# Sums, diagonals and spreads of the turned token groups one block ahead, and the next scaled block in front of the last one's low part

## The chip, the cores and the metric

The kernel runs on one core of a Trainium2 chip. Its time is the device time of one launch in microseconds, the median of several runs. The trace shows one profiled execution of the same program; its span runs from the first to the last instruction, and the launch's own time is a little longer.

## What is computed

One layer of a diffusion backbone: 1024 latent tokens and 256 context tokens of width 1024, all float32. The change works at the very beginning, where tokens are normalised, modulated and multiplied by the first 512 columns of the input projection (the attention values):

```python
m_lat = silu(c) @ w_mod + b_mod          # shift sh1, scale sc1, ... of the latents
m_ctx = silu(c_ctx) @ w_mod + b_mod      # the same for the context
h_lat = rms_norm(x, norm1_g) * (1.0 + sc1) + sh1
h_ctx = rms_norm(ctx, norm1_g) * (1.0 + csc1) + csh1
p_lat = h_lat @ w_in                     # columns split into the heads of retention and attention
p_ctx = h_ctx @ w_in
# retention in two directions, differential attention, output projection, residual,
# then norm, gated MLP with a depthwise convolution, residual, final norm
```

`rms_norm` divides a token by the root of the mean square over its 1024 features.

## The kernel before

Matmul operands are split into a high part, rounded to TensorE's fp32r type, and a low part, the rounding's rest. Each product is three passes: high by high, high by low, low by high (`passes`, L132 to L134; in the first stage L664, L666 and L670 of `part_products`). The modulated tokens stand with features on partitions: eight blocks `d` of 128 features in `hT[0]` (high) and `hT[1]` (low), each in two tiles of 512 tokens; `cT` holds the context.

The 1024 latents come in two ways. **The first 512** (row tiles t=0 to 3) are loaded token by token, scaled by their root, transposed on TensorE for each block (`modulate`, L570), and modulated with high part on ACT (L573), a copy `tmp` on DVE (L575) and the low part on DVE or GpSimd (L577). **The rest** is loaded already turned, features on partitions, in three groups `g` of 256 tokens: g=0 and 1 are latents 512 to 1023, g=2 is the context. For such a group the squares must be summed over partitions, and the result spread over all of them:

- `squares(g, i)`: ACT squares half of the group's eight blocks (L585, 128x1024).
- `over_blocks(g)`: DVE adds the eight blocks up in three steps (L589, L590, L591).
- `over_rows(g)`: TensorE sums over partitions against a tile of ones (`ss`, L596), DVE takes the mean (L114), GpSimd the power −0.5 (L115).
- `halves(g)`: DVE multiplies the identity by those numbers, two diagonal matrices (`diag`, L604).
- `spread(g)`: TensorE multiplies ones by the diagonals, so each partition gets every token's factor (`rp`, L608), and ACT copies that to `rr` (L609).
- `turned` (L611 on), for each block `d`: DVE scales the block by the modulation and by `rr` (L615, to `tmp` where d is even, to `u` where it is odd), ACT adds the shift and rounds (`hi`, L616). Where d is odd, ACT also adds the shift in place (L618) and GpSimd subtracts (L619); where d is even, DVE does both in one operation (`lo`, L621).

The main loop runs over the eight blocks `k` of 128 features. For each it multiplies tiles t=0, 1 (`part_products((0, 1), k)`), then tiles 2, 3, with five PSUM tiles in turn, and the calls around them prepare the blocks to come. After it, tiles t=4, 5 are multiplied block by block, with the helper `between(t, k)` behind each block: it prepares group 1 (at t=4) and the context (at t=5). Tiles 6, 7 and the context's two tiles follow (`natural`), and then block 5 of the projection, whose weights are loaded, split by ACT (L188) and DVE (L189), in four slices of two feature blocks.

Everything from `begin` to `in_order(begin)` keeps its written order on TensorE, DVE, ACT and SP: each instruction there is tied to the one before it on its engine. GpSimd and all later code are placed by the scheduler, which may also put later instructions between the tied ones. Every engine runs its queue in order, so one that waits holds back all behind it. SP issues the loads and stores; the `wr` pool has two buffers for raw weights, and `st`, from which results are stored, has two.

Of the kernel before, what the change touches and what calls it, by code (L numbers as in the profile page):

```python
# [68 lines left out]
def r32(ap):  # L69
    return ap.bitcast(F32)  # L70
# [3 lines left out]
def kernel(  # L74
# [80 lines left out]
    with ExitStack() as p1:  # L155
# [371 lines left out]
        with ExitStack() as p0:  # L527
# [83 lines left out]
            def turned(src, g, d, who, hi, lo):  # L611
# [5 lines left out]
                if d % 2:  # L617
                    nc.scalar.activation(u, u, AF.Identity, bias=sh)  # L618
                    nc.gpsimd.tensor_tensor(out=lo, in0=u, in1=r32(hi), op=ALU.subtract)  # L619
                else:  # L620
                    nc.vector.scalar_tensor_tensor(out=lo, in0=u, scalar=sh, in1=r32(hi), op0=ALU.add, op1=ALU.subtract)  # L621

            def turned_latents(g, d):
# [3 lines left out]
            def context(d):  # L627
                turned(xc[d // 4][:, d % 4, :], 2, d, 1, cT[0][:, d, :], cT[1][:, d, :])
# [5 lines left out]
            rr = xp.tile([P, 3, GQ], F32, name="rr")  # L634
            sqs, diag = {}, {}

# [88 lines left out]
            for k in range(KD):  # L725
# [19 lines left out]
                if k == 4:  # L745
                    over_rows(0)
                if k == 5:
                    spread(0)
                    squares(1, 0)
                if k >= 6:  # L750
                    turned_latents(0, 3 * k - 16)
                    turned_latents(0, 3 * k - 15)
                if k == 7:
                    halves(1)
                if 0 < k < 5:
# [12 lines left out]
                if 0 < k < KD - 2:  # L768
                    mod_sums(k + 2)
                    latents(k + 2)  # L770
                    if 0 < k < 5:
                        for q in range(2):
                            mod_part(k + 3, q)
                        mod_row(k + 3)
                if k in (0, 2, 4):
                    w_split()
                if k == 2:
                    squares(0, 0)
                if k == 4:
                    halves(0)  # L780
                if k == 5:
# [3 lines left out]
                    for i in range(2):  # L785
                        xc.append(xp.tile([P, 4, GQ], F32, name="xc", tag="wt", bufs=5))
                        turned_load(2, i)
                    squares(1, 1)
                    turned_latents(0, 0)
                    turned_latents(0, 1)  # L790
                    over_blocks(1)
                if k >= 6:
                    turned_latents(0, 3 * k - 14)
                if k == 6:
                    over_rows(1)
                if k == 7:
                    spread(1)
            rtab = load_rope(1)
# [3 lines left out]
            def between(t, k):  # L802
# [9 lines left out]
                if t == 5:  # L812
# [6 lines left out]
                    for d in ((k - 4,), range(3, KD))[k == 7] if k > 3 else ():  # L819
                        context(d)  # L820

            for t in (4, 5):
# [899 lines left out]
```

## Time and profile before

| what | us |
|---|---|
| median of 3 runs | 1397.24 (1396.67 to 1398.96) |
| the profiled execution | 1396.65 |
| its span | 1394.9 |
| TensorE busy | 1364.0 (98%) |
| DVE busy | 1003.7 (72%) |
| ACT busy | 743.1 (53%) |
| GpSimd busy | 305.3 (22%) |
| first stage, to the first matmul of block 5 of the projection | 101.0, TensorE busy 87.5 of it |

In the lines of the profile PE is TensorE's matmul, PEld its weight load, POOL is GpSimd, SPq is SP's queue of issues. A line of the timeline has the start, the duration, engine, source line, operation and tiles, and in brackets how long the engine was idle before it and whose result ended that. TensorE's clock can be granted in part; it is given as a share of full speed. Matmuls are pipelined, so that the starts count and not the ends.

### The profile page before, as it was taken

To read this page: it belongs to the slowest core of one execution; us is meant where nothing else is said; L and a number is where in the kernel's file an instruction comes from. 1 tells how busy PE (TensorE), PEld (TensorE's weight loads), DVE (VectorE), ACT (ScalarE), POOL (GpSimd) and SP (SyncE) were. 2 spreads that over 40 slices of the span, in tenths; PEclk is the share of its full clock that TensorE was granted. 3 is DMA by queue.
4 is the path that set the end of the run, shared out by engine and by line. 5 is a ranking of instruction groups with operands and counts; after the bars stand their busy time and mean duration, and the time that the engine had idled before them with its cause. 6 is when DMAs were issued, how large, how long until landed. Compare 5 with 4: busy or idle time off the path is not lost. (4 is left out here: it accounts for less than half of the span.)

```text
span 1394.9 us, 19443 instructions
## 1 busy us (share of the span) xinstructions
PE 1364.0 (98%) x7012; PEld 1144.9 (82%) x7012; DVE 1003.7 (72%) x1494; ACT 743.1 (53%) x1420; POOL 305.3 (22%) x326
## 2 busy tenths in 40 slices
PE   8899999999999999999999999999999999999997
PEld 6678788888888799998888788888888888888886
DVE  4655975434676788896357997887778877799757
ACT  4554413333675699997136655555445555455543
POOL 1220000001656323411201642223332220000001
PEclk9999999999999999999999999999999999999999
DMA  9427886364463787731510223323323225963523
GB/s 379 180 90 240 274 285 213 137 193 153 129 200 132 208 201 166 129 85 52 206 69 31 91 106 114 113 95 109 108 104 113 90 79 179 371 229 105 178 91 129
DMA packets 94761, 214.63 MB, mean 154 GB/s; under 512 B 9220, under 2 KB 29188, under 8 KB 94152
## 3 DMA queue, kind: packets, MB, share of 16 engines
q1 hardware_dynamic: 85928, 186.90, 39.0%
q0 software_dynamic: 8160, 24.91, 7.8%
q10 hardware_dynamic: 576, 1.57, 0.3%
q8 instruction: 55, 0.90, 0.3%
q14 instruction: 42, 0.34, 0.1%
HBM read 158.03 MB, written 55.31 MB: 153 GB/s over the span
## 5 line engine op out<-in xcount | busy, mean ns | idle before, releaser
L132 PE MATMUL pl<-hT,whi 128*128 128x512 f32 x256 | 105.4, 412 | 0.0
L132 PE MATMUL chain<-T,whi 128*128 128x512 f32 x264 | 103.1, 391 | 1.4 <-ACT ub L1376 0.8
L133 PE MATMUL chain<-T,whi 128*128 128x512 f32 x264 | 102.7, 389 | 0.0
L134 PE MATMUL chain<-T,wlo 128*128 128x512 f32 x264 | 102.4, 389 | 0.0
L134 PE MATMUL pl<-hT,wlo 128*128 128x512 f32 x256 | 100.3, 392 | 0.1
L133 PE MATMUL pl<-hT,whi 128*128 128x512 f32 x256 | 99.9, 390 | 0.0
L954 DVE TENSOR_REDUCE mt<-pA 128x1 f32<-128x1280 f32 x64 | 95.1, 1489 | 3.6 <-PE pA L951 2.7
L951 PE MATMUL pA<-ks,qhl 128*128 128x512 f32 (+1 forms) x384 | 89.5, 369 | 1.8 <-DMA ks<-dk 1.5
L132 PE MATMUL c<-whi,ghl 128*128 128x512 f32 x232 | 90.2, 389 | 0.0
L133 PE MATMUL c<-wlo,ghl 128*128 128x512 f32 x232 | 90.2, 389 | 0.0
L134 PE MATMUL c<-whi,ghl 128*128 128x512 f32 x232 | 90.2, 389 | 0.0
L958 ACT ACTIVATE p<-pA,mt 128x1280 f32<-128x1280 f32 x64 | 85.5, 1336 | 6.0 <-DVE mt L954 5.9
L1122 ACT CAST whi<-cmb 128x512 fp32r<-128x512 f32 x62 | 38.5, 622 | 80.5 <-PE chain L133 64.6
L951 PEld LDWEIGHTS pA<-ks,qhl 128*128 128x128 f32 x384 | 67.7, 189 | 14.3 <-issue 1.9
L1282 POOL TENSOR_TENSOR cmb<-wrb 128x512 f32<-128x512 f32 x19 | 28.7, 1511 | 222.0 <-DMA ad<-tconv 96.6
L983 PE MATMUL pv<-va,aT 128*128 128x128 f32 x640 | 77.0, 275 | 0.1
L983 PEld LDWEIGHTS pv<-va,aT 128*128 128x128 f32 x640 | 73.9, 192 | 0.7 <-DVE yT L1012 0.3
L1122 ACT CAST whi<-wra 128x512 fp32r<-128x512 f32 x55 | 33.8, 622 | 72.7 <-PE third L133 42.3
L1125 DVE TENSOR_TENSOR wlo<-cmb,whi 128x512 fp32r<-128x512 f32 x62 | 58.1, 939 | 20.2 <-ACT whi L1122 20.2
L132 PE MATMUL pn<-whi,hT 128*128 128x512 f32 x160 | 65.1, 407 | 0.5 <-ACT hT L616 0.4
L134 PE MATMUL third<-yT,wlo 128*128 128x512 f32 x168 | 65.4, 389 | 0.0
L133 PE MATMUL third<-yT,whi 128*128 128x512 f32 x168 | 65.4, 389 | 0.0
(347 smaller groups left out, 3865.5 us busy)
## 6 DMA issues: line engine op xcount, KB each, us to landing
wm<-w_mod SPq DMA_DIRECT2D x32, 512.0 KB, 5.2
raw<-w_in SPq DMA_DIRECT2D x27, 512.0 KB, 5.1
wra<-w_up SPq DMA_DIRECT2D x24, 512.0 KB, 3.2
wrb<-w_up SPq DMA_DIRECT2D x22, 512.0 KB, 3.5
W<-w_down SPq DMA_DIRECT2D x44, 256.0 KB, 5.7
ad<-s SPq DMA_DIRECT2D x20, 512.0 KB, 3.4
wra<-ad SPq DMA_DIRECT2D x20, 512.0 KB, 3.4
kvs<-kvg SPq DMA_DIRECT2D x36, 256.0 KB, 3.0
```

The costliest lines, as they stand in the source:

```text
L132: mm(ps, lh, rh, start=first, stop=False, skip_group_check=more)
L133: mm(ps, lh, rl, start=False, stop=False, skip_group_check=more)
L134: return mm(ps, ll, rh, start=False, stop=last, skip_group_check=more)
L951: mm(self.pa[m][:, c0:c1], self.q[:, m, i, qs], self.k[:, m, c0:c1], start=(i == 0), stop=(i == 1))
L954: nc.vector.tensor_reduce(out=self.mt[:, m : m + 1], in_=self.pa[m][:, :LK], axis=AX.X, op=ALU.min)
L958: nc.scalar.activation(self.p[m], self.pa[m][:, :LK], AF.Exp, scale=-1.0, bias=self.mt[:, m : m + 1], accum_out=self.s[:, m : m + 1])
L983: mm(self.pv, self.aT[:, c, :], self.v[:, c, :], start=(c == 0), stop=(c == NKT - 1))
L1122: cast = nc.scalar.copy(hi, src)
L1125: nc.vector.tensor_tensor(out=lo, in0=src, in1=r32(hi), op=ALU.subtract)
L1282: nc.gpsimd.tensor_tensor(out=s1, in0=b1, in1=b2, op=ALU.add)
```

## The change

Two things are done. **The order of the preparation** in the main loop: `halves(0)` goes ahead of the weight split of k=4; both `squares` of group 1 and its `over_blocks` follow directly, ahead of the spread's copy or just behind it; `over_rows(1)` goes from behind tiles 2, 3 of k=6 to ahead of them, `halves(1)` from k=7 to the end of k=6, and `spread(1)` from behind tiles 2, 3 of k=7 to ahead of them. **The low part of an even block** is no longer issued by its own call: it is put in the list `owed`, and the next call of `turned` issues it, behind its own scaling (L615) on DVE. The context's last one is issued by `between` at t=5, k=7.

```diff
@@ turned
                 if d % 2:
                     nc.scalar.activation(u, u, AF.Identity, bias=sh)
                     nc.gpsimd.tensor_tensor(out=lo, in0=u, in1=r32(hi), op=ALU.subtract)
-                else:
+                low_part()
+                if d % 2 == 0:
+                    owed.append((lo, u, sh, hi))
+
+            def low_part():
+                for lo, u, sh, hi in owed:
                     nc.vector.scalar_tensor_tensor(out=lo, in0=u, scalar=sh, in1=r32(hi), op0=ALU.add, op1=ALU.subtract)
+                owed.clear()
@@ main loop, behind part_products((0, 1), k)
                 if k == 5:
+                    squares(1, 1)
                     spread(0)
-                    squares(1, 0)
+                    over_blocks(1)
+                if k == 6:
+                    over_rows(1)
                 if k >= 6:
                     turned_latents(0, 3 * k - 16)
                     turned_latents(0, 3 * k - 15)
                 if k == 7:
-                    halves(1)
+                    spread(1)
@@ main loop, behind part_products((2, 3), k)
+                if k == 4:
+                    halves(0)
                 if k in (0, 2, 4):
                     w_split()
                 if k == 2:
                     squares(0, 0)
                 if k == 4:
-                    halves(0)
+                    squares(1, 0)
                 if k == 5:
...
-                    squares(1, 1)
                     turned_latents(0, 0)
                     turned_latents(0, 1)
-                    over_blocks(1)
                 if k >= 6:
                     turned_latents(0, 3 * k - 14)
                 if k == 6:
-                    over_rows(1)
-                if k == 7:
-                    spread(1)
+                    halves(1)
@@ between, t == 5
                     for d in ((k - 4,), range(3, KD))[k == 7] if k > 3 else ():
                         context(d)
+                    if k == 7:
+                        low_part()
```

How the queues move. DVE, from the last modulation before the first diagonal on (`wlo` at L653/L659 is the split of the own weights, at L189 that of block 5; `mcol` and `tmp<-pt` are the modulation of block 7; `tmp<-xh` and `u<-xh` are scaled blocks of group 0, and `hT<-tmp,mcol,hT` an even block's low part). Before:

```order
L604 TENSOR_SCALAR diag<-ident,sm 128x128 x2
L189 TENSOR_TENSOR wlo<-raw,whi 128x1024
L553 TENSOR_SCALAR mcol<-pm,bsc,cl 128x2
L554 TENSOR_SCALAR mcol<-pm,cl 128x2
L575 TENSOR_SCALAR tmp<-pt,mcol 128x512
L615 SCALAR_TENSOR_TENSOR tmp<-xh_196,mcol,rr 128x256
L621 SCALAR_TENSOR_TENSOR hT_170<-tmp,mcol,hT_168 128x256
L615 SCALAR_TENSOR_TENSOR u<-xh_196,mcol,rr 128x256
L589 TENSOR_TENSOR sqt<-sqt 128x1024
L590 TENSOR_TENSOR sqt<-sqt 128x512
L591 TENSOR_TENSOR sqt<-sqt 128x256
```

Changed:

```order
L604 TENSOR_SCALAR diag<-ident,sm 128x128 x2
L659 TENSOR_TENSOR wlo<-raw,whi 128x1024
L589 TENSOR_TENSOR sqt<-sqt 128x1024
L189 TENSOR_TENSOR wlo<-raw,whi 128x1024
L590 TENSOR_TENSOR sqt<-sqt 128x512
L591 TENSOR_TENSOR sqt<-sqt 128x256
L553 TENSOR_SCALAR mcol<-pm,bsc,cl 128x2
L554 TENSOR_SCALAR mcol<-pm,cl 128x2
L575 TENSOR_SCALAR tmp<-pt,mcol 128x512
L615 SCALAR_TENSOR_TENSOR tmp<-xh_196,mcol,rr 128x256
L615 SCALAR_TENSOR_TENSOR u<-xh_196,mcol,rr 128x256
L626 SCALAR_TENSOR_TENSOR hT_170<-tmp,mcol,hT_168 128x256
```

The diagonal stands ahead of the own split (before, L653 is the row ahead of the first one shown), the three sums stand ahead of the modulation of block 7, and an odd block is scaled ahead of the even one's low part.

TensorE, from tiles 0, 1 of k=6 on (`x2` is one pass for two row tiles; `ss` and `rp` are group 1's sum and spread; the three rows of a block are the three passes). Before:

```order
L670 MATMUL pn<-whi,hT_169 128x512 x2
L596 MATMUL ss<-ones,sqt 128x2 x2
L664 MATMUL pn<-whi,hT_167 128x512 x2
L666 MATMUL pn<-wlo,hT_167 128x512 x2
L670 MATMUL pn<-whi,hT_169 128x512 x2
L664 MATMUL pn<-whi,hT_167 128x512 x2
L666 MATMUL pn<-wlo,hT_167 128x512 x2
L670 MATMUL pn<-whi,hT_169 128x512 x2
L608 MATMUL rp<-diag,ones 128x256
L132 MATMUL pn<-whi,hT_168 128x512
```

Changed:

```order
L676 MATMUL pn<-whi,hT_169 128x512 x2
L596 MATMUL ss<-ones,sqt 128x2 x2
L670 MATMUL pn<-whi,hT_167 128x512 x2
L672 MATMUL pn<-wlo,hT_167 128x512 x2
L676 MATMUL pn<-whi,hT_169 128x512 x2
L670 MATMUL pn<-whi,hT_167 128x512 x2
L672 MATMUL pn<-wlo,hT_167 128x512 x2
L676 MATMUL pn<-whi,hT_169 128x512 x2
L608 MATMUL rp<-diag,ones 128x256
L670 MATMUL pn<-whi,hT_167 128x512 x2
```

Before, the first row ends tiles 2, 3 of k=6, and t=4 follows `rp`; changed, it ends tiles 0, 1 of k=6, and tiles 2, 3 of k=7 follow `rp`. Both stand three passes of two tiles earlier.

SP, from the loads of block 5's slices (`raw`) on (`xc` is the context, `dvd<-st` are the stores of the row tiles, `lp`, `lg`, `dec` are small tables for later stages). Before:

```order
L185 DMA raw<-w_in 128x1024 x3
L581 DMA xc<-xt 128x1024 x2
L222 DMA rtab_692<-rope 128x2x512
L222 DMA rtab_693<-rope 128x2x512
L410 DMA dvd<-st 128x512 x5
L856 DMA lp<-rows 128x256
L857 DMA lg<-rows 128x8
L860 DMA dec<-consts 128x1024
L410 DMA dvd<-st 128x512 x2
L185 DMA raw<-w_in 128x1024
L410 DMA dvd<-st 128x512
```

Changed:

```order
L185 DMA raw<-w_in 128x1024 x2
L581 DMA xc<-xt 128x1024 x2
L222 DMA rtab_692<-rope 128x2x512
L222 DMA rtab_693<-rope 128x2x512
L185 DMA raw<-w_in 128x1024
L410 DMA dvd<-st 128x512 x5
L865 DMA lp<-rows 128x256
L866 DMA lg<-rows 128x8
L410 DMA dvd<-st 128x512 x2
L869 DMA dec<-consts 128x1024
L410 DMA dvd<-st 128x512
L185 DMA raw<-w_in 128x1024
```

The third slice stands behind the context and the rope tables, the fourth behind the eighth store where it stood behind the seventh. No operation is added or taken away; the later stages keep their order but for the tables of the decays next to block 5's first tiles.

More of the change, by code (lines that the diff above doesn't have):

```diff
@@ L634 @@
             rr = xp.tile([P, 3, GQ], F32, name="rr")
-            sqs, diag = {}, {}
+            sqs, diag, owed = {}, {}, []
             def wget(k, c0, c1):
```

## The prediction

> **What bounds the kernel now.** The page gives the span, and the windows by stage give what TensorE (PE) does in it.
>
> ```profile
> span 1394.9 us, 19443 instructions
> ...
> 44.60:46.20 1.60, 0.01 (x1) 0.00 (x0) 1.60 (x4) 0.80 (x1) 0.00 (x0) 1.00 0.00 0
> 51.90:56.00 4.10, 0.00 (x0) 0.00 (x0) 4.03 (x6) 1.01 (x2) 1.17 (x2) 0.95 0.98 367
> 56.00:62.40 6.40, 6.31 (x16) 4.65 (x16) 3.53 (x9) 3.34 (x7) 2.34 (x3) 0.50 0.11 43
> 100.00:150.00 50.00, 50.00 (x268) 43.35 (x267) 32.61 (x58) 23.49 (x53) 0.00 (x0) 1.00 0.73 247
> ```
>
> After the two times come the busy times of PE, weight load, DVE, ACT and POOL, then the granted clock and the DMA share. From 100 us on PE is all but full; the two stretches the change works in are empty on PE and full on DVE, and after the second the clock is 0.50. The waits of 38 to 105 us name what PE lacked:
>
> ```profile
> PE ss L596 <- DVE sqt L591: 4.2, 1, 4.2
> PE rp L608 <- DVE diag L604: 2.3, 2, 1.6
> PE pn L134 <- POOL cT L619: 1.0, 1, 1.0
> PE pn L134 <- POOL hT L619: 0.7, 1, 0.7
> PE pn L132 <- ACT hT L616: 0.4, 1, 0.4
> ```
>
> These are the sums, the diagonals and the low parts of the turned groups: all of them what the change moves. The timeline has them in order:
>
> ```profile
> 43.40 1.05 ACT L651 CAST whi<-raw 128x1024 fp32r<-128x1024 f32 x1
> 43.71 0.69 DVE L577 TENSOR_TENSOR hT<-tmp,hT 128x512 fp32r<-128x512 f32 x1
> 44.48 1.23 DVE L653 TENSOR_TENSOR wlo<-raw,whi 128x1024 fp32r<-128x1024 f32 x1
> 45.63 0.47 DVE L604 TENSOR_SCALAR diag<-ident,sm 128x128 f32<-128x128 f32 x2
> 46.25 0.67 PE L608 MATMUL rp<-diag,ones 128*128 128x256 f32 x2 [1.64 <-DVE diag L604]
> 47.23 1.06 ACT L585 ACTIVATE sqt<-xh 128x1024 f32<-128x1024 f32 x1
> 48.69 0.28 DVE L553 TENSOR_SCALAR mcol<-pm,bsc,cl 128x2 f32<-128x2 f32 x1 [1.45 <-PE pm L552]
> 49.87 1.05 ACT L585 ACTIVATE sqt<-xh 128x1024 f32<-128x1024 f32 x1
> 52.95 1.21 DVE L589 TENSOR_TENSOR sqt<-sqt 128x1024 f32<-128x1024 f32 x1
> 54.19 1.26 DVE L590 TENSOR_TENSOR sqt<-sqt 128x512 f32<-128x512 f32 x1
> 55.49 0.42 DVE L591 TENSOR_TENSOR sqt<-sqt 128x256 f32<-128x256 f32 x1
> 56.06 0.98 PE L596 MATMUL ss<-ones,sqt 128*128 128x2 f32 x4 [4.17 <-DVE sqt L591]
> 63.08 0.70 PE L608 MATMUL rp<-diag,ones 128*128 128x256 f32 x2 [0.71 <-DVE diag L604]
> 63.42 0.58 PE L132 MATMUL pn<-whi,hT 128*128 128x512 f32 x1
> ```
>
> So between 44.6, where PE runs dry, and 63.42, where row tile t=4 starts, 1.64 + 4.17 + 0.71 = 6.5 us are empty.
>
> **Term 1, group 0's diagonal in front of the weight split.** It starts where L653 did, 44.48 for 45.63, and the spread's matmul with it, near 45.1 for 46.25: 1.15 us. The split hides in the wait for the squares, below.
>
> **Term 2, group 1's sums a block ahead.** Both squares now follow the cast of 43.40 on ACT at its pace of 0.95 us, 44.35 and 45.30, done at 46.35, ahead of the spread's copy and block 5's first cast. DVE: diagonal, split until 46.1, first sum 46.4 to 47.6 (1.21), block 5's split until 48.8 (its cast comes after the copy), then 0.7 and 0.42: the sums are done near 50.0. PE reaches them sooner too: rp at 45.1, and then tiles 2, 3 of k=5 and tiles 0, 1 of k=6 bring it to 49.2. It waits 0.9 us where it waited 4.17.
>
> What becomes late instead is block 7's modulation, queued on DVE behind the sums: L553 at 49.9 for 48.69, so its POOL low part follows 2.2 us later as now:
>
> ```profile
> 50.89 1.46 POOL L577 TENSOR_TENSOR hT<-tmp,hT 128x512 fp32r<-128x512 f32 x1 [8.02 <-DVE tmp L575]
> 51.78 0.85 DVE L621 SCALAR_TENSOR_TENSOR hT<-tmp,mcol,hT 128x256 fp32r<-128x256 f32 x1 [0.58 <-ACT hT L616]
> 54.18 0.73 POOL L619 TENSOR_TENSOR hT<-u,hT 128x256 fp32r<-128x256 f32 x1 [1.84 <-ACT u L618]
> ...
> 37.61 0.69 DVE L590 TENSOR_TENSOR sqt<-sqt 128x512 f32<-128x512 f32 x1
> ```
>
> That is 52.1 to 53.6, and the third pass of tiles 0, 1 of k=7 waits 0.8 us for it. The same rows show a price that grows when DVE is packed denser: a DVE operation beside a POOL one is stretched (L590 takes 1.26 us at 54.19, with POOL busy from 54.18, and 0.69 alone; L621 ends at 52.63, 0.28 after POOL's 52.35). Between no stretch and a stop until POOL ends I take the stop, which those two rows are nearer to. From 51.95 DVE runs the scaled block of d=0 (0.4), d=1 (stopped until 53.8), the low part of d=0, the mean (0.1), d=2, d=3, the low part of d=2 behind ACT and POOL (to 56.1), d=4, and the diagonal, 56.5 to 56.95: the spread's matmul at 57.0. PE, done with its first half of k=7 at 54.1, waits 2.9 us. Without the stretch it is 56.2 and 2.1.
>
> "SBUF — State Buffer" of the Trainium skill, section "Who interferes with whom", speaks against the change here: a VectorE instruction with two SBUF inputs and a GpSimd one that reads SBUF exclude each other, and the second stops altogether. The rows above agree within 0.3 us; by the rule the sum is the one I take, without it 0.9 us more is gained.
>
> Without waits PE's work between 44.6 and 63.42 is 18.8 − 6.5 = 12.3 us. In the third window it worked at clock 0.50: ss and 12 matmuls, some 3.4 us at full clock (0.23 each, by the rows of term 3), took 6.4, so 9.3 us are left at full clock. The new start of t=4 is 44.6 + 9.3 + 0.45 (rp) + 0.9 (ss) + 0.8 (low part) + 2.9 (rp) = 59.0: 4.4 us gained, term 1 within it.
>
> **Term 3, the low part behind the next scaled block.** Today DVE stands until ACT has rounded each even block, and PE later stands for DVE's chain:
>
> ```profile
> 72.72 0.39 PE L133 MATMUL pn<-wlo,hT 128*128 128x512 f32 x1
> ...
> 76.89 0.40 PE L132 MATMUL pn<-whi,hT 128*128 128x512 f32 x1
> ...
> 95.56 0.40 PE L132 MATMUL pn<-whi,cT 128*128 128x512 f32 x1
> ...
> 101.02 0.39 PE L132 MATMUL pl<-hT,whi 128*128 128x512 f32 x1
> ...
> 64.86 0.80 DVE L615 SCALAR_TENSOR_TENSOR tmp<-xh,mcol,rr 128x256 f32<-128x256 f32 x1 [1.44 <-ACT rr L609]
> ...
> 86.49 0.47 DVE L615 SCALAR_TENSOR_TENSOR tmp<-xc,mcol,rr 128x256 f32<-128x256 f32 x1
> 88.15 0.66 DVE L621 SCALAR_TENSOR_TENSOR cT<-tmp,mcol,cT 128x256 fp32r<-128x256 f32 x1 [1.19 <-ACT cT L616]
> 89.13 0.47 DVE L615 SCALAR_TENSOR_TENSOR tmp<-xc,mcol,rr 128x256 f32<-128x256 f32 x1
> ```
>
> A row tile is 24 matmuls, 95.56 to 101.02: 5.46 us, 0.2275 each. From 63.42 to 101.02 stand six of them (t=4 to 7, two of context), 32.8 us, and 0.95 for the sums and spread of context; the rest of the 37.6, 3.9 us, is waiting: 72.72 to 76.89 takes 4.17 for eight matmuls (1.8), so 2.35; the context's last low part 1.1; restarts. A pair of blocks now takes DVE 89.13 − 86.49 = 2.64 us, 1.19 of it the wait for ACT. With the next scaled block (0.4) ahead of the low part, DVE's three operations at 0.4 and what is left of the wait make 1.6, ACT's three (0.5, 0.5, 0.42) 1.5; with POOL's stretch up to 1.9. Group 1 then starts at 59.4, when DVE is through with the rest of group 0 (2.4 us from the diagonal on), for 64.86. From there to its sixth block's low part, for which PE waits today until 76.5, is 11.6 us; ACT's four evictions, the wait for their stores and the context's squares lie in it, so I take the denser pairs as worth nothing here: 70.9. PE comes for it at 59.0 + 47 matmuls (10.7) = 69.7 and waits 1.2. Context's blocks are then done near 82 and PE gets there at 82.9: no wait. So 33.8 + 1.2 = 35.0 us in place of 37.6, and the next block starts at 94.0: **7.0 us** gained at that place.
>
> **Term 4, the next block's weights: nothing.** SP's third slice of block 5 moves behind the context's loads and the rope tables, still ten microseconds ahead of the first store. The fourth moves behind the eighth store:
>
> ```profile
> 92.00 0.33 SPq L856 DMA_DIRECT2D lp<-rows  x1
> 95.32 0.45 SPq L185 DMA_DIRECT2D raw<-w_in  x1
> ...
> 103.63 1.23 DVE L189 TENSOR_TENSOR wlo<-raw,whi 128x1024 fp32r<-128x1024 f32 x1
> ...
> PE pg L509 <- DVE xhl L499: 0.5, 2, 0.3
> ```
>
> Its low part ends at 104.86, and PE needs it 20 matmuls into the tile that begins at 101.02, at 105.6. After: SP's lp load follows the last DVE read of the context's tiles, near 82 (92.00 now); sixth to eighth store until 88; then, as now, 8.3 us to the split and 1.2 for it: 97.5. PE needs it at 94.0 + 4.55 = 98.5. Hidden by one microsecond. If SP's hop over the eighth store took the 5.3 us that lie between the slice and that store's issue today, on top of the full 11.6 from lp to split, it would end at 100.1 and cost 1.6.
>
> **Sum.** −4.4 − 2.6 + 0 = −7.0: a span of 1387.9 in place of 1394.9. The profiled execution took 1396.65, 0.6 under the median of the runs, 1397.24; less 7.0 that is **1390.2**. Behind 101 us both kernels run one order but for the decay tables' work up to 130 us, and PE stays full, so the gain arrives at the end. Bounds: with no POOL stretch +0.9 and no wait at 69.7 +1.2, 1388.1; with the whole 2.35 still waited for (1.2 more than I take) and the slice late by 1.6, 1393.0.
>
> **Rivals.**
>
> *The clock halves all the same.* PE waits 0.9, 0.8 and 2.9 us within seven. For: 4.1 us empty left 6.4 us at 0.50. Against: the 1.64 us wait at 46.25 left the clock at 1.00, and today's 4.17 are not reached. Price: half of 6.4, 3.2 us, less the 1.2 that PE would have waited at 69.7 anyway: 1392.2. "TensorE: Matmul & The Clock Gate" of the Trainium skill, section "What's actually happening", halves the clock after an idle window of about 3.4 us; by that rule no wait here is long enough, and this rival would not come.
>
> *The gain is given back behind 101 us.* There DVE adds up the second modulation beside PE, with DMA at 0.73. If those loads or sums ran at their own pace, PE would wait for their turned sums (pg): 1397. Against: pg waits 0.5 us in all, and SP issues those loads behind the stores of PE's results, so they come earlier by as much.
>
> *The change doesn't do what it says.* If the second sum or block 5's cast comes late in the new order (the cast needs the raw slice, the copy the spread), ss ends where it did and only the 1.15 us of the diagonal are won: 1396.1. Against: all inputs, the turned rows of group 1 among them, are used by 49.87 today, and the split of block 5's slice ends before that.
>
> *Slower: the fourth slice behind the eighth store.* That store needs its eviction, this the buffer of the sixth store, and ACT and SP take them in turn; PE's first tile of block 5 stands until the slice is split. It decides once the split ends after 104.86, and each microsecond beyond is one lost: at 107 it is 1399.4. Against: 7.4 us lie between that and my 97.5, and even the longest rows end at 100.1.
>
> **How the numbers follow.** The sum as it stands 0.70 (its own range 1388.1 to 1393.0), the clock 0.16, given back 0.06, not done 0.04, slower 0.04. The forecast is the first: 1390.2. The range takes its bounds and the clock with a microsecond on top, 1388.0 to 1394.2; that leaves out the other three and some of the first. A measurement of this kernel tells 0.2%, 2.8 us, from no change, so faster means under 1394.4: 0.70 + 0.16 = 0.86. Given back and not done are the same, 0.10; slower 0.04.
>
> **What would show it.** Right: rp's first wait near 0.4 us, ss before tiles 2, 3 of k=6 with a wait of about 1, rp's second with 2 to 3, no stretch of clock 0.50 after 50 us, t=4 starting near 59, DVE's pairs at 1.6 to 1.9 us, block 5 at 94. Wrong: rp waits over 3.5 us and the clock falls; block 5 starts at 94 but PE waits in it for wlo; or the start is right and the end is not 7 us earlier.

## The result and the profile after

The changed kernel takes 1395.14 us in the median of 18 runs (1391.41 to 1396.85), the kernel before 1398.11 in 18 runs on the same chips: a ratio of 0.9974, 95% interval 0.9965 to 0.9983. The profiled execution took 1393.87 us with a span of 1392.1. So about 3 us came where 7.0 were forecast, and the time lies outside the range, which ended at 1394.2. Of the kernels further below, c5_start_raw has no trace to read, since the execution that was profiled ran at a mean granted clock of 0.556 and took 2293.23 us.

The windows of the changed kernel, with the columns of the prediction's windows, cover the wait for the second spread, what follows it, and a stretch near 457 us, far behind the change:

```profile
54.40:57.50 3.10, 0.00 (x0) 0.00 (x0) 2.84 (x7) 2.33 (x5) 2.43 (x3) 1.00 0.60 238
57.50:58.50 1.00, 0.95 (x3) 0.84 (x3) 1.00 (x3) 0.51 (x1) 0.00 (x0) 0.53 0.00 0
58.50:61.00 2.50, 2.50 (x7) 1.95 (x6) 2.03 (x5) 2.38 (x6) 0.95 (x2) 0.50 0.02 7
61.00:64.00 3.00, 3.00 (x14) 2.47 (x14) 1.27 (x3) 1.73 (x5) 0.52 (x1) 1.00 0.45 175
...
457.00:460.30 3.30, 3.30 (x10) 2.70 (x9) 1.49 (x1) 0.67 (x1) 1.26 (x2) 0.50 1.03 336
```

PE stands idle for 3.1 us, and then the clock is 0.50 for 3.4 us; near 457, behind a wait of 1.84 us, it is 0.50 again. PE's waits over the whole trace (total, times, longest):

```profile
PE rp L608 <- DVE diag L604: 3.5, 2, 3.2
PE pA L960 <- DMA ks<-dk: 1.8, 1, 1.8
...
PE pg L509 <- DVE xhl L499: 1.1, 2, 1.0
...
PE ss L596 <- DVE sqt L591: 0.8, 1, 0.8
...
PE pg L509 <- ACT xhl L498: 0.5, 1, 0.5
...
PE pn L676 <- POOL hT L577: 0.5, 1, 0.5
PE pl L134 <- DVE wlo L189: 0.3, 1, 0.3
```

The waits of 72 to 96 us for low parts are gone. New are the long wait of `rp`, and 1.6 us at `pg`, the turned sums of the second modulation, where it was 0.5. The wait of `pA`, the first attention scores, is the one near 457; it was 1.52 before. The 0.3 us for `wlo` lie at 329 us and have nothing to do with block 5's slices: between 94.70 and 150 PE waits nowhere for 0.1 us. The timeline of the steps:

```profile
45.06 0.67 PE L608 MATMUL rp<-diag,ones 128*128 128x256 f32 x2 [0.33 <-DVE diag L604]
...
50.14 0.58 PE L596 MATMUL ss<-ones,sqt 128*128 128x2 f32 x4 [0.82 <-DVE sqt L591]
52.11 1.46 POOL L577 TENSOR_TENSOR hT<-tmp,hT 128x512 fp32r<-128x512 f32 x1 [9.12 <-DVE tmp L575]
52.34 1.51 DVE L615 SCALAR_TENSOR_TENSOR u<-xh,mcol,rr 128x256 f32<-128x256 f32 x1
53.62 0.73 PE L676 MATMUL pn<-whi,hT 128*128 128x512 f32 x2 [0.47 <-POOL hT L577]
56.56 0.94 DVE L604 TENSOR_SCALAR diag<-ident,sm 128x128 f32<-128x128 f32 x2
57.55 1.22 PE L608 MATMUL rp<-diag,ones 128*128 128x256 f32 x2 [3.20 <-DVE diag L604]
61.07 0.39 PE L132 MATMUL pn<-whi,hT 128*128 128x512 f32 x1
...
77.36 0.49 DVE L615 SCALAR_TENSOR_TENSOR tmp<-xc,mcol,rr 128x256 f32<-128x256 f32 x1 [1.36 <-ACT rr L609]
78.83 0.48 DVE L615 SCALAR_TENSOR_TENSOR tmp<-xc,mcol,rr 128x256 f32<-128x256 f32 x1
80.50 0.47 DVE L615 SCALAR_TENSOR_TENSOR tmp<-xc,mcol,rr 128x256 f32<-128x256 f32 x1
...
94.70 0.39 PE L132 MATMUL pl<-hT,whi 128*128 128x512 f32 x1
```

Row by row this is the forecast up to 57.55, within 0.6 us; t=4 starts at 61.07 in place of 59.0, and block 5 at 94.70 (forecast 94.0, before 101.02). The gain there is 6.3 us. A pair of context blocks takes DVE 1.47 and 1.67 us (77.36 to 78.83 to 80.50) where it took 2.64. Matching PE's matmuls one to one, the lead over the kernel before is 6.2 us at 89 us, 4.9 behind `pg`, 4.5 behind the transposes at 275 us, and 3.05 behind the stretch of 457 us and at the end. So in this execution most of the gain is made by block 5, as forecast, and half of it is lost again at places the forecast called untouched.

The first such place is `pg`. ACT's second rounding of the turned context (`xhl<-pc`, L417) needs a buffer that a store (`dk<-xhl`) frees. The changed kernel first, SP's issues under SPq:

```profile
109.44 1.46 SPq L185 DMA_DIRECT2D raw<-w_in  x2
109.52 0.37 ACT L417 CAST xhl<-pc 128x256 fp32r<-128x256 f32 x1
111.18 7.70 SPq L419 DMA_DIRECT2D dk<-xhl  x3
117.50 0.38 ACT L417 CAST xhl<-pc 128x256 fp32r<-128x256 f32 x1 [7.61 <-DMA dk<-xhl]
...
127.28 0.67 SPq L480 DMA_DIRECT2D macc<-rows  x1
130.69 1.29 DVE L482 SCALAR_TENSOR_TENSOR macc<-wm,csil,macc 128x1024 f32<-128x1024 f32 x1 [0.75 <-DMA macc<-rows]
...
150.42 0.50 PE L509 MATMUL pg<-xhl,one_r 128*128 128x512 f32 x1 [0.49 <-ACT xhl L498]
...
151.88 0.50 PE L509 MATMUL pg<-xhl,one_r 128*128 128x512 f32 x1 [0.97 <-DVE xhl L499]
```

The kernel before:

```profile
116.91 0.33 SPq L185 DMA_DIRECT2D raw<-w_in  x1
117.52 1.26 SPq L419 DMA_DIRECT2D dk<-xhl  x2
118.98 0.82 SPq L185 DMA_DIRECT2D raw<-w_in  x1
122.10 0.38 ACT L417 CAST xhl<-pc 128x256 fp32r<-128x256 f32 x1 [4.73 <-DMA dk<-xhl]
...
131.88 0.67 SPq L480 DMA_DIRECT2D macc<-rows  x1
135.34 1.29 DVE L482 SCALAR_TENSOR_TENSOR macc<-wm,csil,macc 128x1024 f32<-128x1024 f32 x1 [0.80 <-DMA macc<-rows]
...
156.81 0.50 PE L509 MATMUL pg<-xhl,one_r 128*128 128x512 f32 x1 [0.34 <-DVE xhl L499]
```

With two raw loads ahead of the store the rounding comes 6.3 us after the store's issue, with one 4.6. So it comes 22.8 us behind block 5's start, where it came 21.1 behind: 1.7 us later. SP issues the load `macc<-rows`, with which the sums of the second modulation begin, behind the stores: it leaves 32.6 us behind block 5's start in place of 30.9, the first sum on DVE starts at 36.0 in place of 34.3, and the last of them, rounded for `pg` (`xhl`, L499), ends at 57.1 in place of 55.7.

### The profile page after: what moved, and what is told of

Same layout as the page of the kernel before. It is cut to its first block, busy times and chain, and to the rows that moved or that the text cites. A ratio compares the mean times of both kernels' runs of the same rounds, so it can differ in the third digit from the quotient of the medians.

```text
span 1392.1 us, 19443 instructions
## 1 busy us (share of the span) xinstructions
PE 1364.0 (98%) x7012; PEld 1146.0 (82%) x7012; DVE 1007.0 (72%) x1494; ACT 743.4 (53%) x1420; POOL 304.3 (22%) x326
## 5 line engine op out<-in xcount | busy, mean ns | idle before, releaser
L133 PE MATMUL third<-yT,whi 128*128 128x512 f32 x168 | 65.4, 389 | 0.0
L132 PE MATMUL third<-yT,whi 128*128 128x512 f32 x168 | 65.4, 389 | 0.0
```

The source lines that it names most:

```text
L132: mm(ps, lh, rh, start=first, stop=False, skip_group_check=more)
L133: mm(ps, lh, rl, start=False, stop=False, skip_group_check=more)
```

## The experiments

The first runs take the change apart, the next fill PE's idle times with matmuls whose results nobody uses, and the last move single operations to see what holds up `pg`. Where a few operations are added, the planner (the scheduler that places the later code) can move others too; what it moved is said with each run. All times of the table but the medians come from the profiled executions, in us; "from rp" means from the first spread's start, which leaves out what happens before the change's place. "xhl" is the second `xhl<-pc` after block 5's start; "idle" is PE's idle time at `pg`. Ratios are to the kernel before in the same comparison.

| kernel | rp, second, from rp | t=4 from rp | block 5 from rp | clock 0.50 in 53 to 70 | xhl | idle | median | ratio (95%) |
|---|---|---|---|---|---|---|---|---|
| before | 16.83 | 17.18 | 54.77 | 6.83 | 21.1 | 0.5 | 1398.11 | 1 |
| changed | 12.50 | 16.01 | 49.65 | 3.41 | 22.8 | 1.6 | 1395.14 | 0.9974 (0.9965–0.9983) |
| e1_order | 14.37 | 17.94 | 54.72 | 6.83 | 17.6 | 0 | 1396.94 | 0.9993 (0.9983–1.0002) |
| e2_owed | 14.52 | 14.76 | 49.33 | 3.41 | 22.5 | 4.5 | 1395.07 | 0.9985 (0.9969–1.0001) |
| e3_busy | 12.62 | 14.50 | 49.43 | 0 | 19.1 | 0 | 1390.70 | 0.9947 (0.9934–0.9960) |
| e4_raw | 12.49 | 16.06 | 50.89 | 6.83 | 19.4 | 0.3 | 1392.96 | 0.9965 (0.9952–0.9977) |
| e5_behind | 12.50 | 12.85 | 48.33 | 3.41 | 18.5 | 0 | 1390.54 | 0.9943 (0.9929–0.9956) |
| e9_alone | 12.62 | 14.51 | 49.43 | 0 | 20.6 | 0 | 1392.21 | 0.9957 (0.9944–0.9970) |
| e13_start | 12.63 | 14.52 | 49.44 | 0 | 19.0 | 0 | 1389.17 | 0.9939 (0.9927–0.9952) |
| c1_before_busy | 16.77 | 17.09 | 54.91 | 3.41 | 16.0 | 0 | 1395.35 | 0.9981 (0.9972–0.9990) |
| c3_after_start | 12.50 | 16.08 | 50.49 | 6.83 | 22.0 | 1.4 | 1393.62 | 0.9964 (0.9952–0.9977) |
| c4_order | 12.61 | 14.51 | 49.39 | 0 | 20.8 | 0.1 | 1389.69 | 0.9938 (0.9926–0.9951) |
| c5_start_raw | – | – | – | – | – | – | 1392.27 | 0.9961 (0.9949–0.9972) |
| e14_best | 12.61 | 12.93 | 48.02 | 0 | 20.1 | 0 | 1390.41 | 0.9941 (0.9927–0.9955) |
| d1_lg_first | 12.50 | 16.08 | 50.44 | 6.83 | 21.8 | 1.8 | 1394.00 | 0.9967 (0.9955–0.9978) |
| d2_lg_last | 12.62 | 14.52 | 49.41 | 0 | 21.7 | 1.1 | 1390.59 | 0.9951 (0.9937–0.9964) |

### Each half alone

e1_order issues the low part in its own call again:

```diff
-                low_part()
                 if d % 2 == 0:
                     owed.append((lo, u, sh, hi))
+                low_part()
```

> The changed kernel with the low part of an even block issued in its own call again: the new order of sums, diagonals and spreads alone. Theory A (order and owed low part help at different places, and block 5 is bound by group 1's blocks): ss comes near 50.1 as in the changed kernel, the second diagonals are 1 to 2 us later, near 58, because each even block of group 0 holds DVE for ACT's rounding; PE then waits over 4 us ahead of the second spread and its clock halves for two windows; group 1's pairs take 2.6 us, and block 5 starts at 96.5 to 98 (101.02 before, 94.70 with the whole change). Time 1 to 2 us below the kernel before, ratio 0.9985 to 0.9993. Theory B (the order alone carries the gain, the owed low part is hidden): block 5 near 95 and a ratio of 0.9975.

e2_owed is the kernel before with `owed` and `low_part` as in the change, every other call at its old place.

> The kernel before with the owed low part alone: DVE takes the next scaled block in front of the last even block's low part, the order of sums, diagonals and spreads as before. Theory A: PE's wait of 4.17 us ahead of ss and its half clock stay (DVE's sums come behind two blocks of group 0 as before, the low part of block 0 now behind block 1's scaling); t=4 starts 0.5 to 1.5 us earlier than 63.42, group 1's and the context's pairs take 1.5 to 1.7 us and the waits of 72 to 96 shrink from 3 us to under 1; block 5 starts at 97.5 to 99. Time 1 to 2 us below the kernel before, ratio 0.9985 to 0.9993. Theory B (the owed low part is hidden, since PE waits elsewhere): block 5 at 100.5 to 101, ratio 1.000.

PE's waits in e1_order, 42 to 105 us, and the window behind the second spread:

```profile
PE rp L608 <- DVE diag L604: 5.4, 2, 5.1
PE pn L134 <- POOL cT L619: 1.6, 1, 1.6
...
61.70:66.30 4.60, 4.53 (x11) 3.57 (x12) 2.26 (x6) 3.10 (x8) 1.07 (x2) 0.50 0.02 4
```

PE's waits in e2_owed, whole trace:

```profile
PE ss L596 <- DVE sqt L591: 4.0, 1, 4.0
PE pg L509 <- ACT xhl L498: 3.6, 1, 3.6
```

From the first spread to block 5, the order alone takes 54.72 us, no less than the kernel before (54.77), and the owed low part alone 49.33, as little as both (49.65). The order moves PE's 4.17 us wait from the sums to the second spread, where it is 5.06 because each even block holds DVE, and the clock halves as before; expectation A, 96.5 to 98 for block 5, was too good (102.13; 2.3 us of that come from an early stretch of half clock before the first spread, at 11.8 to 18.6). What the order brings is the first spread 1.2 us earlier, as the changed kernel has it. e2_owed did better in this stage than expected: 97.76 for block 5 lies in the expected 97.5 to 99 only because its first spread came 2.2 us late, behind an early half clock too, and from there on it is 2 us or more faster than that. But it waits 4.5 us at `pg`, and its time (0.9985) cannot be told from e1_order's. Its `xhl` is as late as in the changed kernel (22.5 for 22.8), yet its sums end 3.1 us later behind block 5; why is not shown.

### The clock at the second spread, and what else filling it moved

e3_busy:

```diff
+            def keep_busy(n):
+                idle = pst.tile([P, 512], F32, name="idle", tag="tr")
+                for _ in range(n):
+                    mm(idle, lat_lhs(0, 0)[0], wget(7, 0, 512)[0], start=True, stop=True)
...
                 if k == 7:
+                    keep_busy(13)
                     spread(1)
```

> The changed kernel with 13 matmuls more, whose results are not used, ahead of the second spread, so that PE is busy while it waits for group 1's diagonals (54.35 to 57.55). The planner also places a few of the decay tables' operations on ACT and DVE otherwise; the end result is the same. Both theories: no window of clock 0.50 near 57, and tile t=4 starts near 59.3 where it started at 61.07. Theory A (group 1's blocks on DVE, ACT and POOL set the start of block 5 whatever PE does at 57): PE now waits about 1.2 us for them near 70, and block 5 starts at 94.2 to 94.7 as in the changed kernel; the time falls by 0 to 0.6 us. Theory B (the half-clock window is what the forecast lacks): block 5 starts at 93.0, and the time falls by 1.7 us: a ratio to the kernel before near 0.9962.

```profile
57.60:58.50 0.90, 0.86 (x4) 0.79 (x5) 0.90 (x3) 0.51 (x1) 0.00 (x0) 1.00 0.00 0
58.50:61.00 2.50, 2.50 (x13) 2.06 (x12) 2.04 (x5) 2.38 (x6) 0.95 (x2) 1.00 0.03 7
```

These are the windows of e3_busy: the clock is whole, and PE does 13 matmuls in the 2.5 us in which it did 7. Block 5 stands where A put it, 94.45. The time, though, fell by 3.8 us (0.9974 to 0.9947), more than either theory had: `pg` waits for nothing any more. That was taken for ACT's order, which the planner had changed with the added matmuls. e9_alone ties ACT to the changed kernel's order:

```diff
+            for e in exps:                          # decay tables' exponentials
+                order_only(e.ins, sts[-1].ins)      # behind the context's last eviction
...
+            for e in exps:
+                order_only(cast.ins, e.ins)         # casts of the following weights
```

> The 13 matmuls ahead of the second spread as in e3_busy (their results are not used), but with ACT held to the changed kernel's order: the decay tables behind the context's last eviction, the casts of the following weights behind the last of them. Theory A (two parts: the halved clock costs block 5 only 0.3 to 1.6 us, because group 1's blocks set its start anyway, and the rest of what e3_busy won comes from ACT's order, by which the raw loads left SP before the stores of the turned context): no clock of 0.50 near 57, block 5 at 94.2 to 94.7, the second xhl<-pc again some 22.5 us behind block 5's start, idle time of 1 to 2 us on PE at pg, and a ratio to the kernel before of 0.9962 to 0.9970. Theory B (all of what e3_busy won is the clock): a ratio near 0.9947 as e3_busy, and no idle time at pg.

0.9957 lies between the two, with an interval that overlaps that of e3_busy. PE does not wait at `pg`, although the raw loads again leave SP ahead of the stores (97.82 to 108.57, the stores from 108.85): the reason given under A did not hold as put. e4_raw tries SP's order by itself:

```diff
+            if late_load:                           # slices 3 and 4 of the following weights
+                order_only(load.ins, first_stores[1].ins)
```

> The changed kernel with one edit: SP issues the raw loads of slices 3 and 4 of the next block of weights behind the second store of the turned context (dk<-xhl) and not ahead of the first. Theory A (the new order of SP's queue gives back part of the gain: ACT's second rounding of the context, xhl<-pc, waits for a store of dk that stands behind two raw loads, and the sums of the second modulation in front of pg come late with it): the second xhl<-pc starts near 116.3 in place of 117.5, the lag to the kernel before stays at 6.0 or more up to pg near 151, PE waits at pg 0.5 us or less in all where it waited 1.5, and the time falls by 1.0 to 1.4 us below the changed kernel's: a ratio to the kernel before near 0.9966 for its 0.9974. Theory B (what is missing is all the half-clock window after the second spread, and the rest chance): no change, 0.9974, and the idle time at pg stays. Theory C (the sums in front of pg are bound by their own loads of the modulation weights): xhl<-pc comes earlier, pg does not.

```profile
112.30 1.26 SPq L423 DMA_DIRECT2D dk<-xhl  x2
113.64 1.25 SPq L187 DMA_DIRECT2D raw<-w_in  x2
115.46 0.37 ACT L421 CAST xhl<-pc 128x256 fp32r<-128x256 f32 x1 [4.45 <-DMA dk<-xhl]
```

The rounding comes 3.2 us after the store's issue in place of 6.3, and the idle time at `pg` falls to 0.3, as A had it. PE also comes to block 5 1.2 us later here (50.89 from rp, two halved windows), which by itself leaves less to wait for; but c3_after_start and d1_lg_first below come as late, without the moved loads, and wait 1.4 and 1.8 us. For the same reason the lead at block 5 is 5.0 us and not the 6.0 of A. In time e4_raw looked like A (0.9965), but its interval holds the changed kernel's 0.9974 too; see c5_start_raw.

e5_behind puts the second spread back behind tiles 2 and 3 of k=7:

```diff
-                if k == 7:
-                    spread(1)
...
                 if k == 6:
                     halves(1)
+                if k == 7:
+                    spread(1)
```

> The changed kernel with the second spread put back behind tiles 2 and 3 of k=7, the rest of the change kept. The planner then also issues the raw loads of slices 3 and 4 of the following weights behind the second store of the turned context. Theory A (the place of the spread is the mistake in the change: PE has 2.8 us of work at that place that does not need it, and the loads ahead of the stores cost 1.2 us): PE waits for the second spread under 1 us, no clock of 0.50 near 57, t=4 starts near 58.3 (61.07 in the changed kernel), block 5 at 94.2 to 94.7, no idle time over 0.6 us at pg, and a ratio to the kernel before of 0.994 to 0.996, as e3_busy without its added matmuls. Theory B (the spread is better ahead: what follows it on ACT and DVE starts earlier): group 1's blocks start later, block 5 at 95.5 or later, and a ratio of 0.997 or more.

```profile
PE rp L608 <- DVE diag L604: 2.1, 2, 1.8
...
58.80:62.10 3.30, 3.30 (x10) 2.52 (x9) 2.27 (x5) 3.21 (x8) 1.47 (x2) 0.50 0.00 0
```

The time is as A had it: with no added work the kernel reaches 0.9943, whose interval stands clear of the changed kernel's. t=4 is 3.2 us earlier from rp than in the changed kernel, and block 5 starts 48.33 from rp, at 93.51 (94.2 to 94.7 was expected). A missed the wait and the clock: PE still waits 1.8 us (under 1 was expected), and even that halved the clock. Since the planner moved the raw loads behind the second store as well, the gain is that of both moves.

### The idle times elsewhere

e13_start is e3_busy, c3_after_start the changed kernel, with `turn_over(9)` ahead of `mod_part(0, 1)` made `turn_over(17)`; c1_before_busy is the kernel before with that and 17 matmuls ahead of `over_rows(1)`.

> e3_busy with 8 more pairs of matmuls of ones in the row that keeps PE busy before the second half of the first modulation block (idle 8.57 to 10.25 there); their results are not used, as those of the row now. Theory A (idle times of 1.5 us and more halve the clock in some executions, by where they lie against the windows of 3.41 us; two of six profiles had 0.50 from about 11.5 to 18 and reached the first spread 2.2 us later): no such window, runs spread less, and the median falls 0.3 to 1.0 us below e3_busy's: ratio near 0.9942. Theory B (those windows have another cause): same ratio, 0.9947, and some executions still have them.

> The changed kernel with only the 8 more pairs of matmuls of ones at the start (results not used); every other instruction in the same order. Theory A (three places lose: the start by chance, the second spread always, the first scores by chance): the start's windows are gone, the one near 57 stays; the median falls by 0.5 to 1.0 us below the changed kernel's, ratio 0.9967 to 0.9971. Theory B (the windows of the start do not matter): ratio 0.9974.

> The kernel before with matmuls in its idle times, whose results are not used: 8 more pairs of ones ahead of the second half of the first modulation block, and 17 ahead of group 1's sums (ss), where PE waits 4.17 us. The planner places a few of the decay tables' operations and the following weights' casts otherwise. Theory A (in the kernel before DVE's sums and blocks set the pace from 52 to 96 us, so the half clock of 55.62 to 62.45 costs nearly nothing there, while the scattered windows of half clock elsewhere cost 1.7 us each and fall on the kernel before as on the changed one): no clock of 0.50 before 400 us, block 5 at 100 to 101, a ratio to the kernel before of 0.998 to 0.9995. Theory B (a good part of what the changed kernel won is that it freed PE of the half clock, and matmuls alone do that): block 5 near 97.6, a ratio of 0.9970 or less.

All five runs of e13_start have a mean granted clock of 0.998 or 0.999 and lie within 1.5 us, as A had it, though its ratio (0.9939) lies within the interval of e3_busy's; the changed kernel's 18 runs have 0.993 to 0.997 and lie within 5.4. At the same 0.997 four runs of it took 1391.41 to 1393.32, at 0.993 three took 1395.13 to 1396.85. c3_after_start gained 1.4 us (0.9974 to 0.9964, with intervals that overlap), and its trace still halves the clock at the second spread. In c1_before_busy block 5 is no earlier (54.91 from rp), as A had it; the ratio 0.9981 is at the good end of A's range. A's "no clock of 0.50 before 400 us" was wrong: once the sums' wait is filled, the second spread waits, and the clock halves behind it.

```profile
PE rp L608 <- DVE diag L604: 5.4, 2, 3.7
...
65.00:68.30 3.30, 3.30 (x10) 2.52 (x9) 2.08 (x4) 2.08 (x6) 0.73 (x1) 0.50 0.41 159
```

### What is left between c3_after_start and the filled kernels

c4_order is e9_alone with the filled start, c5_start_raw is c3_after_start with e4_raw's order, e14_best is e5_behind with the filled start and 7 matmuls ahead of the second spread.

> e9_alone (13 matmuls whose results are not used ahead of the second spread, ACT held to the changed kernel's order) with the 8 more pairs at the start: PE is kept busy as in e13_start, and the two differ only in the order in which ACT and DVE take the decay tables and the following weights' splits. Theory A (that order costs by itself, since the raw loads leave SP ahead of the turned context's stores): 0.4 to 1.2 us above e13_start, ratio 0.9943 to 0.9948. Theory B (with the clock whole that order costs nothing): same as e13_start, 0.9939.

> The changed kernel with the 8 more pairs of matmuls of ones at the start (results not used) and SP's order of e4_raw (raw loads of slices 3 and 4 of the following weights behind the second store of the turned context), nothing else moved. The halved clock at the second spread stays. Theory A (what the changed kernel lacks is three things: the windows of the start, the loads ahead of the stores, and the halved clock at the second spread, about 1.4, 1.2 and 2.4 us): 1.2 us below c3_after_start, a ratio to the kernel before of 0.9953 to 0.9958, no idle time over 0.5 us at pg. Theory B (the loads ahead of the stores cost nothing that arrives at the end; e4_raw was lucky in its windows): 0.9964, as c3_after_start, with the time lost again behind pg.

> e5_behind (second spread behind tiles 2 and 3 of k=7 again) with the idle times filled: the 8 more pairs at the start, and 7 matmuls ahead of the second spread (results not used). The planner places the decay tables' operations otherwise again. Theory A (the place of the spread and the whole clock add up): PE waits under 0.5 us for the second spread, no clock of 0.50 before 400 us, t=4 starts near 58.0, block 5 at 93.0 to 93.6 (93.51 in e5_behind with a half clock, 94.44 in e13_start), ratio 0.9928 to 0.9938. Theory B (group 1's blocks set block 5's start, whatever PE does): block 5 at 94.4 and a ratio of 0.9939 as e13_start.

c4_order equals e13_start (0.9938), as B had it. c5_start_raw (0.9961) stays nearer B (0.9964) than A (0.9953 to 0.9958), and its interval holds both, so it is not shown that the loads ahead of the stores cost the end anything; in e4_raw's trace PE waits 0.83 us just ahead of 234.18 us instead, at the transposes. e14_best has block 5 1.4 us earlier from rp than e13_start, and the time is no better (0.9941).

Two last kernels move the last step of the decay rates (`lg`, L898) against the split of block 5's fourth slice on DVE, first without, then with filled idle times:

```diff
+            order_only(splits[-1].ins, lg_step.ins)      # d1_lg_first, on c3_after_start
...
+            order_only(acc_step.ins, splits[-1].ins)     # d2_lg_last, on c4_order
```

> c3_after_start (the changed kernel with the start filled by 8 more pairs of matmuls of ones, results not used) with one edit: on DVE the last split of the weights of block 5 (wlo of slice 4) comes behind the last step of the decay rates (lg), not ahead of it. The planner then also runs the decay tables' exponentials on ACT earlier, four of them ahead of the context's last eviction. Theory A (the wait at pg and pk comes from this: both splits stand ahead of lg on DVE, so ACT's decay tables, the following weights' casts, their loads and the turned context's stores are all late): the second xhl<-pc at 19 to 20 us behind block 5's start in place of 22.0, no idle time over 0.5 us at pg, 1.2 to 1.7 us below c3_after_start: a ratio to the kernel before of 0.9952 to 0.9956. Theory B (what c3_after_start lacks against c4_order is only the halved clock at the second spread): 0.9964.

> c4_order (PE kept busy at the start and ahead of the second spread) with one edit: on DVE both last splits of the weights of block 5 come ahead of the last two steps of the decay rates (lg), as in the changed kernel. Theory A (this order gives back part of the gain at pg): lg 1.2 to 1.4 us later against block 5's start, PE idle at pg for 0.7 to 1.5 us, and 1.0 to 1.5 us above c4_order: ratio 0.9946 to 0.9949. Theory B (the order costs nothing while the clock is whole): 0.9938 as c4_order.

d2_lg_last, SP, ACT and PE:

```profile
108.49 1.47 SPq L189 DMA_DIRECT2D raw<-w_in  x2
...
110.23 8.00 SPq L425 DMA_DIRECT2D dk<-xhl  x4
116.19 0.37 ACT L423 CAST xhl<-pc 128x256 fp32r<-128x256 f32 x1 [7.25 <-DMA dk<-xhl]
...
150.85 0.50 PE L515 MATMUL pg<-xhl,one_r 128*128 128x512 f32 x1 [0.89 <-DVE xhl L505]
```

d2_lg_last went as A: with block 5 at the same place from rp (49.41 and 49.39) and the clock whole in both, `xhl` is 0.9 us later than in c4_order, PE is idle for 1.1 us at `pg` where it was 0.1, and the median is 0.9 us higher (1.8 by the ratios, whose intervals overlap). d1_lg_first went as B: the exponentials start earlier, but the raw loads still leave SP right ahead of the stores, `xhl` stays at 21.8, and nothing is gained. Over all traces one relation holds: PE waits over 1 us at `pg` in the five kernels where `xhl` comes more than 21.5 us behind block 5, and 0.5 or less in the ten where it comes sooner. What makes it late is several things, of which no single one was shown to decide.

## Why the prediction was wrong

- **Term 1** was right: the first spread at 45.06, forecast near 45.1.
- **Term 2, the waits**, was right in each row to about half a microsecond: `ss` at 50.14 with 0.82 (50.0, 0.9), block 7's low part with 0.47 (0.8), the second spread at 57.55 after 3.20 (57.0, 2.9). DVE stopped until POOL was done, as taken: 1.51 us for a 0.4 us operation.
- **The step that failed first** is "9.3 us are left at full clock". The rival "The clock halves all the same", given 0.16, is what happened. It was turned down because the 4.17 us of the kernel before were not reached; 3.20 were enough, and so were 1.82 in e5_behind. t=4 came at 61.07, not 59.0: 0.5 us by the later spread, most of the rest by the halved clock.
- At block 5 the total came near, 6.3 for 7.0, but partly because two errors offset each other: t=4 was 2.1 us late, and from there to block 5 it took 33.6 us and not 35.0, since the 1.2 us that PE was to wait for group 1 near 70 did not come (the price of the rival had counted on that). There was luck in it too. Three other traces with the same wait of 3.2 us (e4_raw, c3_after_start, d1_lg_first) have two halved windows for the one of the changed kernel's, by where the grid of these windows lay (last section), and block 5 at 50.44 to 50.89 from rp, against 49.65 with one and 49.43 with none (e3_busy).
- **The division between terms 2 and 3** was wrong. The sum gave the order 3.25 us beyond term 1 and the owed low part 2.6; from rp to block 5, the order alone gave nothing and the owed low part alone all of it. Term 2's working already runs DVE through group 0 with the next scaled block ahead of the low part, so its 3.25 us belong to both edits. The reason given for term 3, that DVE stands until ACT has rounded, holds ahead of the second diagonals too, and there the sum credits the order with it.
- **"The gain arrives at the end"** is the step that took the time out of the range. The rival "given back behind 101 us", given 0.06, has the place right, but not the way: the sums did not run at their own pace, their first load left SP late, behind the stores of the turned context. "They come earlier by as much" was the reason against it, and it held for all but 1.7 us. In the profiled executions 1.3 us went at `pg`, 0.5 at 275 us, and 1.4 at 457 us, where a wait of 1.84 halved the clock and the 1.52 of the kernel before did not. 6.3 − 1.3 − 0.5 − 1.4 is the 3.1 that is left.
- **The base** was one execution of the kernel before with one halved stretch, where DVE set the pace. Its 18 runs have a median 0.9 us above the three shown, and filling its idle times gains 2.7 us (c1_before_busy). With idle times filled in both, the change is worth 0.9938 / 0.9981 = 0.9957, or 6.0 us, near the forecast; unfilled, about 3. The two are not quite alike, though: in c1_before_busy the second spread still waits 3.7 us and halves the clock once, in c4_order it does not. Against the filled kernel, the changed one lacks 5.0 us by the ratios: 1.4 by the start (c3_after_start), 1.8 from there to d2_lg_last by the second spread's wait, 1.8 from there to c4_order by the late order at `pg`. Each of these has an interval of about as much; only their sum stands clear of it, so how it divides is not shown.
- "Slower" and "not done" did not come. Block 5's fourth slice was hidden, as term 4 had it: PE does not wait for it.
- Two slips in the working changed nothing: by its own rows the stretch is worth 0.8 us (57.0 for 56.2), not 0.9, and a microsecond on top of 1393.0 is 1394.0, not 1394.2.

## What to carry to other kernels

A wait of PE is to be priced with the clock behind it: here 1.8 us of idle time within one window of 3.4 mostly halved it for the next one or two. Work that does not need the awaited result belongs in front of the wait (e5_behind reaches 0.9943 by moving one call, with the loads that the planner moved along). When two edits are made at once, each is to be run alone, since their terms can overlap. A trace is one execution: the same wait halved one window in one and two in others. And a gain of six microseconds meets the next chain that has no slack, here `pg` with 0.5 us of waiting before; its margin is to be worked out like a term of the sum.

## What the runs showed of the hardware

- The stretches of half clock, but for the one at the very end of each trace, last 3.413 or 6.827 us, and in each trace they start a whole number of 3.413 us apart (57.57 and 456.93 in the changed kernel: 117 of them). Where this grid lies against the program differs from run to run. With the grid laid over PE's idle times in the 15 traces read, from the first granted full clock to 1375 us, 17 windows at full clock had PE idle for 1.76 us or more, and 16 of them were followed by half clock (the other, 1.89 us at the start of e5_behind, was not); 14 windows had 1.26 to 1.67 us idle, and none of them was. So a wait counts by what of it falls into one window: 2.42 us at the first attention scores in e4_raw split in two (0.93 and 1.49) and did nothing, 1.84 at the same place in the changed kernel lay in one and halved the clock. How long the half clock lasts went by the window after that: it ended after 3.413 us in the nine stretches where PE worked through it (at most 0.06 us idle), and lasted 6.827 in the seven where PE stood for 0.43 to 2.16 us in its first half, since the wait reached into it or others followed. "TensorE: Matmul & The Clock Gate" of the Trainium skill, section "What's actually happening", has a free-running window of 3413 ns, with which the grid agrees, and throttles after an idle window; here windows in which PE worked for almost half the time (1.65 of 3.413 us) were idle enough.
- Eight pairs of matmuls whose result nobody reads, put into 1.7 us of idle time at the start, go with steadier times: the seven traced kernels that have them spread over 1.5 to 3.5 us, the eight without them over 2.1 to 11.2 (5 to 18 runs each). The two sets overlap.
